# Down projection of a two-layer encoder's FFN: tokens stationary, 512-column weights moving, and a turn of the rows

## The chip, the cores and the metric

The kernel runs on one core of one Trainium2 chip. The metric is the time of one execution on the device in microseconds (us). The engines are named as in the profile: PE is TensorE (matmuls), PEld its loads of stationary tiles, DVE is VectorE, ACT is ScalarE, POOL is GpSimd, which here issues DMAs that add to what lies at their target, and SP is SyncE, which issues the other DMAs.

## What is computed

An encoder of two residual layers over 512 tokens with 1024 features, in float32. Layer 0 mixes tokens by gated linear attention, layer 1 by softmax attention, and each layer ends in a gated FFN with 2816 hidden features and a convolution of width 3 along the tokens. The change touches the FFN's last product alone.

```python
def conv_ffn(h, w_up, w_conv, b_conv, w_down):
    u = h @ w_up                                  # 512 x 1024 by 1024 x 5632
    u = lax.conv_general_dilated(u, w_conv[:, None, :], window_strides=(1,), padding=[(1, 1)],
        dimension_numbers=('NWC', 'WIO', 'NWC'), feature_group_count=u.shape[-1]) + b_conv
    val, gate = jnp.split(u, 2, axis=-1)
    return (jax.nn.silu(gate) * val) @ w_down     # 512 x 2816 by 2816 x 1024

for i in range(DEPTH):                            # DEPTH = 2
    x = x + mixer_i(rmsnorm(x, norm_mix[i]))
    x = x + conv_ffn(rmsnorm(x, norm_ffn[i]), w_up[i], w_conv[i], b_conv[i], w_down[i])
```

## The kernel before

**Number format.** Each float32 operand is split into a high part, rounded to the format that TensorE reads (`wh`, `xt`, `nh`, the first half of a `gu`), and a low part, the rest (`wl` and the others). A product is three matmuls: high by high, high by low, low by high. For a weight ScalarE makes the high part (`wh<-raw`) and VectorE the low part (`wl<-raw,wh`). For the strips named in `LOW_0`, `LOW_1` and `LOW_2`, ScalarE writes the negated high part into `wl` and a DMA on POOL's queue adds the weights to it (`low_dma`), so that VectorE does nothing.

**Layout.** x is kept with features on partitions, 8 chunks of 128 features by 512 tokens (`x[0]` to `x[7]`). In the FFN, x goes to DRAM (`x_home`, tiles `xd`) and its buffers (tag "x") then hold weights, from chunk m = 1 on (`WIDE_AT`) until it comes back (`x_load`, at `BACK_AT` = 20).

**Loops.** `ffn` walks the 22 chunks m of 128 hidden features. `act_up(m)` makes the two up projections, the convolution and the gate. Chunks 4 to 21 are multiplied "by seven" (`SEVEN`): the operands are cut into 2 x 2 blocks, and seven products of sums of blocks take the place of eight. The down projection adds over the hidden features, so it is done in pieces when their gates are there: `down_part` for chunks 0 to 7 within m = 9 and for chunks 8 to 15 within m = 17 (`DOWN_AFTER`), `tail_part` for 16 to 19 behind m = 21, and the two last chunks without the scheme (`rest`). Tokens are cut in two halves of 256 for it; `prepare` makes from two chunks the seven token sums and splits them into `gu` tiles.

**`down_part` before.** For each of four strips n of output features (`NQ`), `product` runs seven products, each over four pairs of chunks with three matmuls, so 7 x 4 x 3 x 4 = 336 in a part. A weight tile of 128 x 128 is stationary and 256 tokens move: 128 x 256 into a half of a PSUM buffer. A strip's weights come in three pieces (`Weights.summed`), whose sums VectorE makes: lines L335, L344 and L346 in the profile, with splits at L338 and L375. ScalarE doubles, negates and copies partial results between PSUM buffers (L1222, L1299, L1309, L1317); VectorE adds them (`add_seven`); the finished 128 x 512 tiles `f` and `g` are added to `x_home` by POOL's DMAs.

**Queues and order.** `Weights.todo` is the list of weight pieces in the order of use. `piece` takes the next one and prepares up to `PA` or `PAW` (4 or 6) pieces ahead; `ahead` issues the loads of the next 3 on SP (`LOADS`). `flush` issues on POOL the adding DMAs that are pending. The order on each engine is fixed when the program is built: a scheduler takes the instructions by rank (`tc.high_priority(n)` raises it) and by when their operands come. PSUM has buffers with the tags "acc", "pt" and "s", two each in these parts, and one "po".

**Behind layer 0's FFN.** `tail_part` finishes the output features in two pairs of strips. `end(c, ...)` adds a finished chunk to `x[c]` on VectorE (L1382), and `nxt.chunk(c)` then starts the next layer's norm for it (`xhl` on ScalarE L520, its low part on VectorE L525, the square on ScalarE L529). ScalarE's negated copies for the second pair of strips are lines L1354 and L1369. In layer 1, `end` stores the output.

## Time and profile before

| what | before |
|---|---|
| median of 3 runs (lowest to highest) | 1075.08 us (1074.94 to 1075.72) |
| the profiled execution's own time | 1075.15 us |
| its span, first to last instruction | 1073.4 us |
| ScalarE's busy share | 73% |
| GpSimd's busy share | 15% |
| mean DMA rate over the span | 163 GB/s |

A group's row reads: line, engine, operation, output<-inputs, shapes, count | busy time in all and the mean of one in ns | idle time ahead of them and what ended it. A matmul's duration counts its whole passage, and several are under way at once; their pitch, the time from one start to the next, is the time that each adds. A chain row reads: start, length, engine, output, line, count. A row of a timeline: start, duration, then the instructions, with idle time ahead in brackets. A window's row: its bounds and length, then PE, PEld, DVE, ACT and POOL busy (instructions), the granted clock, the DMA engines' share and GB/s.

In the profile of before, the down parts of layer 0 lie at about 325 to 365 us and 446 to 487 us, and layer 0's tail at about 542 to 555 us.

### The profile page before, as it was taken

The page shows a single profiled execution, that of the slowest core. Times are in us where ns is not written, and L with a number is a line of the kernel's source. Part 1 is how long each engine was busy: PE and PEld are TensorE (multiplying, and loading weights), DVE is VectorE, ACT ScalarE, POOL GpSimd, SP SyncE. Part 2 cuts the span into 40 slices and gives each one's busy share as a digit, 9 for nine tenths or more (in the row PEclk, how much of TensorE's full clock was granted, in tenths as well). Part 3 has the DMA queues.
Part 4 walks back from the last instruction along what each step waited for, and adds up shares of the span by engine and source line. Part 5 has one row for each costly group of instructions (what it writes and reads, how often), then busy time and mean ns, then how long its engine had stood idle before and what let it go on. Part 6 is the DMA issues. An engine that isn't in the chain of part 4 may idle for free.

```text
span 1073.4 us, 18685 instructions
## 1 busy us (share of the span) xinstructions
PE 1064.8 (99%) x7176; PEld 981.2 (91%) x7176; DVE 940.8 (88%) x1423; ACT 784.1 (73%) x1252; POOL 157.0 (15%) x169
## 2 busy tenths in 40 slices
PE   9999999999999999999999999999999999999998
PEld 8888988888999999999988888788899999999997
DVE  7998968888999999999985578787899999999995
ACT  8679665757886788776784677675888777876783
POOL 0212112011101110010015343001201021001000
PEclk9999999999999999999999999999999999999999
DMA  8844447666554874484668565486756487456562
GB/s 292 193 133 100 116 145 259 223 134 127 147 147 124 208 186 124 117 182 124 225 165 208 123 201 167 148 265 142 143 129 159 115 201 196 125 130 155 149 194 82
DMA packets 75322, 174.57 MB, mean 163 GB/s; under 512 B 6880, under 2 KB 7392, under 8 KB 75232
## 3 DMA queue, kind: packets, MB, share of 16 engines
q1 hardware_dynamic: 50624, 114.23, 31.6%
q0 software_dynamic: 19712, 50.60, 27.1%
q10 hardware_dynamic: 4896, 8.55, 2.2%
q8 instruction: 56, 0.92, 0.3%
q14 instruction: 34, 0.28, 0.1%
HBM read 124.85 MB, written 14.68 MB: 130 GB/s over the span
## 4 chain that ended last, share of the span: by engine, by line
PE 95%; DVE 3%; ACT 1%; DMA 0%; issue 0%; DVEq 0%; ACTq 0%
PE r L1153 52%; PE op L608 8%; PE vg L733 5%; PE up L556 3%; PE up L557 3%; PE up L555 3%; PE kq L665 2%; PE av L582 1%; PE A L555 1%; PE A L557 1%; PE B L557 1%; PE A L556 1%; PE B L555 1%; PE B L556 1%; PE pt L1613 1%; PE o L979 1%
## 5 line engine op out<-in xcount | busy, mean ns | idle before, releaser
L1153 PE MATMUL r<-xt,wh 128*128 128x256 f32 x1152 | 208.0, 282 | 0.0
L1153 PE MATMUL r<-gu,wh 128*128 128x256 f32 x1120 | 202.1, 283 | 0.7 <-ACT r L1369 0.7
L375 DVE TENSOR_TENSOR wl<-raw,wh 128x1024 fp32r<-128x1024 f32 x146 | 176.2, 1217 | 19.3 <-ACT wh L374 18.8
L1153 PEld LDWEIGHTS r<-xt,wh 128*128 128x128 f32 x1152 | 178.9, 191 | 0.2
L374 ACT ACTIVATE wh<-raw 128x1024 fp32r<-128x1024 f32 x146 | 151.1, 1052 | 36.6 <-DVE raw L346 8.3
L1153 PEld LDWEIGHTS r<-gu,wh 128*128 128x128 f32 x1120 | 173.6, 190 | 1.9 <-ACT r L1369 1.1
L1153 PE MATMUL r<-xt,wl 128*128 128x256 f32 x576 | 162.8, 283 | 0.0
L1153 PE MATMUL r<-gu,wl 128*128 128x256 f32 x560 | 156.7, 283 | 0.0
L1153 PE MATMUL r<-nh,wh 128*128 128x256 f32 x432 | 122.6, 284 | 0.0
L1153 PE MATMUL r<-nh,wl 128*128 128x256 f32 x432 | 122.0, 282 | 0.0
L1153 PE MATMUL r<-nl,wh 128*128 128x256 f32 x432 | 121.7, 282 | 0.0
L1153 PEld LDWEIGHTS r<-xt,wl 128*128 128x128 f32 x576 | 109.7, 190 | 0.0
L1153 PEld LDWEIGHTS r<-gu,wl 128*128 128x128 f32 x560 | 106.1, 190 | 0.0
L1153 PEld LDWEIGHTS r<-nh,wh 128*128 128x128 f32 x432 | 82.1, 190 | 0.6
L1153 PEld LDWEIGHTS r<-nl,wh 128*128 128x128 f32 x432 | 82.1, 190 | 0.1
L1153 PEld LDWEIGHTS r<-nh,wl 128*128 128x128 f32 x432 | 82.1, 190 | 0.0
L374 ACT ACTIVATE wh<-sum 128x1024 fp32r<-128x1024 f32 x56 | 59.2, 1056 | 24.1 <-DVE sum L344 17.6
L608 PE MATMUL op<-oT,wh 128*128 128x512 f32 x256 | 72.6, 393 | 0.0
L375 DVE TENSOR_TENSOR wl<-sum,wh 128x1024 fp32r<-128x1024 f32 x56 | 68.2, 1217 | 3.8 <-ACT wh L374 3.8
L324 ACT ACTIVATE wh<-raw 128x1024 fp32r<-128x1024 f32 x46 | 48.4, 1051 | 17.2 <-PE A L556 6.7
L344 DVE TENSOR_TENSOR sum<-raw,raw 128x1024 f32<-128x1024 f32 x50 | 60.8, 1216 | 0.0
L608 PEld LDWEIGHTS op<-oT,wh 128*128 128x128 f32 x256 | 47.4, 188 | 9.7 <-ACT oT L1018 0.3
(304 smaller groups left out, 2577.6 us busy)
## 6 DMA issues: line engine op xcount, KB each, us to landing
raw<-in_w_up_dram SPq DMA_DIRECT2D x78, 512.0 KB, 5.1
raw<-in_w_down_dram SPq DMA_DIRECT2D x44, 512.0 KB, 4.0
wl<-raw POOLq DMA_DIRECT2D x20, 512.0 KB, 5.7
wl<-in_w_up_dram POOLq DMA_DIRECT2D x20, 512.0 KB, 6.6
ring<-p ACTq DMA_DIRECT2D x32, 256.0 KB, 2.6
xw<-in_xw_dram SPq DMA_DIRECT2D x8, 512.0 KB, 6.8
raw<-in_w_v_dram SPq DMA_DIRECT2D x8, 512.0 KB, 4.5
raw<-in_w_g_dram SPq DMA_DIRECT2D x8, 512.0 KB, 4.0
```

The costliest lines, as they stand in the source:

```text
L324: act.activation(hi, r, AF.Copy)
L344: dve.tensor_tensor(fold(e), t3[:, :S].rearrange("p (o n) -> p o n", o=1).to_broadcast([P, 2, S]), fold(tiles[0]), ALU.add)
L374: act.activation(hi[:, sl], a, AF.Copy)
L375: dve.tensor_tensor(lo[:, sl], a, hi[:, sl].bitcast(F32), ALU.subtract)
L555: mm(ps, wh, mh, start=start, stop=False, **kw)
L556: mm(ps, wh, ml, start=False, stop=False, **kw)
L557: return mm(ps, wl, mh, start=False, stop=stop, **kw)
L582: mm(ps[j][:, :width], hl[k][i == 2][:, j * P : (j + 1) * P], (wl if i == 1 else wh)[:, sl], start=k == 0 and i == 0, stop=k == KC - 1 and ...
L608: mm(pss[ng][n], wt[:, sl], mv, start=k == late[0][0] and i == 0, stop=k == late[-1][-1] and i == 2)
L665: mm(ps[t], (wl if i == 1 else wh)[:, kk * S + t * P : kk * S + (t + 1) * P], norm.hl[k][i == 2], start=k == 0 and i == 0, stop=k == KC - ...
L733: last = mm(ps[j], m[:, js], w[:, sl], start=i in (1, 7, 2) and p == 0 and a == 0, stop=i in (4, 2, 3) and p == 3 and a == 2, skip_group_c ...
L1153: mm(dst, w[:, sl], m, start=start and j == 0 and a == 0, stop=j == len(pairs) - 1 and a == 2, skip_group_check=True)
```

## The change

**Down parts.** `down_part` now multiplies with tokens stationary and weights moving. `rows(i, ps, start, hf)` runs one of the seven products over one half hf of the pairs: for two pairs, two groups j of 128 tokens and three terms, a 128 x 128 tile of `gu` is stationary and 512 columns of a weight piece move, into a whole PSUM buffer of 128 tokens by 512 output features. A part has 7 x 2 x 2 x 2 x 3 = 168 matmuls. The seven products stand in the order 1, 7, 6, 4, 5, 2, 3 (`DOWN_ORDER`); the partial results are `ya` (tag "acc"), `yb` ("pt") and `yc` ("s"), and the finished ones `e`, `f` and `g`, which POOL's DMAs store to `y_home` (tiles `yd`, 128 tokens by 1024 features): written by part 0, added by part 1.

**Their weights.** A part has 14 pieces of 128 x 1024 in place of the strips' sums. `load_rows` loads raw blocks as whole rows; `make_rows` adds two of them on VectorE for products 7, 6, 5 and 3 and splits each piece. The two raw tiles of product 1 are in "x" buffers. `_layout` puts the weights in that order ahead of the launch.

**Turning back.** At m = 18 (`Y_AT`) `turn_back` loads the four `yd` tiles on SP. From m = 20 on (`BACK_TURNS`) it gives `product` eight steps, one of which runs after each product: four transposes of 128 x 128 on TensorE into one PSUM buffer `yt` (tag "po"), a copy on ScalarE into `x[c]` at rank 200, and after every second step a DMA on POOL that adds `x_home` to the pair of chunks. The loads of `x_home` into x at m = 20 are gone.

**Behind layer 0.** In `tail_part`, the norm's steps `nxt.chunk(c)` for c = 2 and 3 are kept in `later` and issued behind the next pair's negated copies. The additions in `end` have rank 200 (`END_RANK`).

**Low parts by DMA.** `LOW_0` loses 13 and gains 14 and 16, so one more strip of the up projection in each layer has its low part made by a DMA. `OP_FIRST` and `ROW_DMA` are empty, so what they govern does nothing.

**What moved: the start of part 0 in layer 0.** On TensorE, before, where the first of the part's matmuls stands; r_3231 is the up projection of m = 9, r_3359 the part's first strip and r_3414 the next up projection:

```order
L1153 MATMUL r_3231<-nh_2232,wl_3140 128x256
L1153 MATMUL r_3359<-gu_2374,wh_3211 128x256 x2
L1153 MATMUL r_3414<-gu_2374,wh_3245 128x256 x2
L1153 MATMUL r_3414<-gu_2374,wl_3246 128x256
L1153 MATMUL r_3414<-gu_2575,wh_3245 128x256
L1153 MATMUL r_3359<-gu_2374,wl_3212 128x256
L1153 MATMUL r_3359<-gu_2575,wh_3211 128x256 x2
```

and of the change, where r_3233 is the up projection of m = 9 and ya_3341 the part's first result:

```order
L1202 MATMUL r_3233<-xt_2476,wl_3103 128x256
L1363 MATMUL ya_3341<-wh_3164,gu_2376 128x512
L1202 MATMUL r_3233<-nh_2215,wh_3070 128x256
L1202 MATMUL r_3233<-nl_2216,wh_3070 128x256
L1202 MATMUL r_3233<-nh_2215,wl_3071 128x256
L1363 MATMUL ya_3341<-wl_3165,gu_2376 128x512
L1363 MATMUL ya_3341<-wh_3164,gu_2376 128x512
L1363 MATMUL ya_3341<-wh_3164,gu_2577 128x512
L1363 MATMUL ya_3341<-wl_3165,gu_2577 128x512
```

The matmuls are twice as wide, and the part's first piece (wh_3164, wl_3165) is read among the last products of m = 9.

SP's queue, before, with the loads of part 0 in layer 0:

```order
L270 DMA raw_3070<-in_w_down_dram 128x2x512
L273 DMA raw_3071<-in_w_down_dram 128x2x512
L270 DMA raw_3215<-in_w_down_dram 128x2x512
L273 DMA raw_3216<-in_w_down_dram 128x2x512
L270 DMA raw_3343<-in_w_down_dram 128x2x512
L273 DMA raw_3344<-in_w_down_dram 128x2x512
```

and of the change, where raw_3074 and raw_3106 are product 1's two tiles, in "x" buffers:

```order
L277 DMA raw_3147<-in_w_down_dram 128x1024
L277 DMA raw_3168<-in_w_down_dram 128x1024
L277 DMA raw_3219<-in_w_down_dram 128x1024
L277 DMA raw_3252<-in_w_down_dram 128x1024
L277 DMA raw_3074<-in_w_down_dram 128x1024
L277 DMA raw_3106<-in_w_down_dram 128x1024
L277 DMA raw_3348<-in_w_down_dram 128x1024
```

The pieces used first are loaded fifth and sixth, behind those for products 7 and 6.

**What moved: the turn at m = 20.** TensorE before, in the last products of m = 20 in layer 0, where nothing stands between them:

```order
L1153 MATMUL r_5705<-nh_2225,wl_5558 128x256
L1153 MATMUL r_5705<-nh_2232,wh_5557 128x256
L1153 MATMUL r_5705<-nl_2233,wh_5557 128x256
L1153 MATMUL r_5705<-nh_2232,wl_5558 128x256
L1153 MATMUL r_5705<-nh_2211,wh_5614 128x256
```

and of the change, with the third and fourth group of transposes:

```order
L1223 MATMUL yt_5426<-ident,y_5091 128x128
L1202 MATMUL r_5457<-nh_2229,wh_5244 128x256
L1202 MATMUL r_5457<-nl_2230,wh_5244 128x256
L1202 MATMUL r_5457<-nh_2229,wl_5245 128x256
L1202 MATMUL r_5457<-nh_2236,wh_5244 128x256
L1202 MATMUL r_5457<-nl_2237,wh_5244 128x256
L1202 MATMUL r_5457<-nh_2236,wl_5245 128x256
L1202 MATMUL r_5316<-nh_2215,wh_5168 128x256
L1223 MATMUL yt_5444<-ident,y_5088 128x128
L1223 MATMUL yt_5444<-ident,y_5089 128x128
```

Seven matmuls lie between these two groups, which share one PSUM buffer.

**What moved: layer 0's tail.** ScalarE before, where the negated copies of the second pair of strips stand (r_6218 and r_6226):

```order
L1222 ACTIVATE f_6242<-r_6228 128x512
L337 ACTIVATE wh_6150<-raw_5908 128x512
L1222 ACTIVATE f_6252<-r_6245 128x512
L520 ACTIVATE xhl_6177<-x_5758,prm 128x512
L1369 ACTIVATE r_6218<-r_6168 128x256
L1354 ACTIVATE r_6226<-r_6203 128x256
L520 ACTIVATE xhl_6190<-x_5758,prm 128x512
```

and of the change (r_5865 and r_5873):

```order
L1447 ACTIVATE r_5873<-r_5850 128x256
L569 ACTIVATE xhl_5875<-x_5381,prm 128x512
L1296 ACTIVATE f_5901<-r_5887 128x512
L1296 ACTIVATE f_5911<-r_5904 128x512
L569 ACTIVATE xhl_5881<-x_5381,prm 128x512
L376 ACTIVATE wh_5852<-raw_5768 128x1024
L375 ACTIVATE wl_5853<-raw_5768 128x1024
L375 ACTIVATE wl_5889<-raw_5817 128x1024
L1465 ACTIVATE r_5865<-r_5827 128x256
L1465 ACTIVATE r_5873<-r_5850 128x256
```

The first two copies (L1354 before, L1447 now) stand ahead of the norm's steps (L520, now L569), and the second two (L1369, now L1465) stand together, no longer right behind one of those steps.

The diff, cut to its core:

```diff
@@ -61,6 +61,11 @@
 NQ, NPART = 4, 2
+DOWN_ORDER = (1, 7, 6, 4, 5, 2, 3)
+BACK_TURNS = 20
+Y_AT = 18
+TURN_RANK = 200
 NTAIL = 2
@@ -89,7 +94,7 @@
-LOW_0 = (5, 6, 7, 8, 9, 13, 15, 17)
+LOW_0 = (5, 6, 7, 8, 9, 14, 15, 16, 17)
@@ -104,6 +109,8 @@
 UPAW = 3
+END_RANK = 200
@@ -260,9 +267,51 @@
+        def load_rows(self, src, n, h):
+            part, i = divmod(n, 10)
+            q, key = {1: 0, 7: 1, 6: 2, 5: 1, 2: 3}.get(i), (id(src), n, h)
+            if q is None or key in self.loaded:
+                return
+            self.loaded[key] = t = pair("x", KC // 2, F32, "raw") if i == 1 else pair("raw", NR, F32, "raw")
+            sync.dma_start(t, src[part * NQ + 2 * h + q // 2, :, q % 2 * 2 * S : (q % 2 + 1) * 2 * S])
+        def make_rows(self, src, n, h):
+            self.load_rows(src, n, h)
+            at = lambda i: (id(src), n // 10 * 10 + i, h)
+            put = lambda a, b: dve.tensor_tensor(a, a, b, ALU.add)
+            i, raws = n % 10, self.loaded
+            if i in (1, 2):
+                r = raws[at(i)]
+            elif i in (7, 6):
+                r = raws[at(1)]
+                put(r, raws[at(i)])
+                if i == 7:
+                    del raws[at(7)]
+            elif i == 4:
+                r = raws[at(6)]
+            elif i == 5:
+                r = raws.pop(at(5))
+                put(r, raws.pop(at(6)))
+            else:
+                r = raws.pop(at(2))
+                put(r, raws.pop(at(1)))
+            hi, lo = self.two()
...
+                self.split(hi, lo, r)
+            return hi, lo
         def load(self, key):
             src, i, h = key
-            if i < 0:
+            if i <= -100:
+                self.load_rows(src, -i - 100, h)
+            elif i < 0:
                 self.load_vg(src, -i, h)
@@ -416,10 +468,7 @@
             add_up(layer, range(first, m + 1))
-            W.add(down_w[layer], range(part * NQ, (part + 1) * NQ), 4)
-            at = len(W.todo) - 4 * NQ - 1
-            if m not in SEVEN:
-                W.todo[at : at + 2] = W.todo[at + 1], W.todo[at]
+            W.todo += [(down_w[layer], -100 - 10 * part - i, h) for i in DOWN_ORDER for h in range(2)]
             first = m + 1
@@ -1153,6 +1202,31 @@
             W.flush()
+            if turning:
+                turning.pop(0)()
+        y_home, turning = [dp.tile([P, D], F32, tag=nm("yd"), name=nm("yd")) for _ in range(NT)], []
+        def turn_back():
+            W.flush()
+            y = [big(F32R, "y") for _ in range(NT)]
+            for t, home in zip(y, y_home):
+                sync.dma_start(t.bitcast(F32), home)
+            tiles = []
+            def turned(c):
+                if not tiles:
+                    tiles.extend(x_tiles())
+                ps = bank("po", "yt")
+                for t in range(NT):
+                    pe.transpose(ps[:, t * P : (t + 1) * P].bitcast(F32R), y[t][:, c * P : (c + 1) * P], identr)
+                with tc.high_priority(TURN_RANK):
+                    act.activation(x[c], ps, AF.Copy)
+                if c % 2 == 1:
+                    pool.dma_start(tiles[c // 2], x_home[c // 2], accum_op=ALU.add)
+            return [lambda c=c: turned(c) for c in range(KC)]
@@ -1277,9 +1351,70 @@
             pairs = [quads.pop(part * NQ + i) for i in range(NQ)]
-            st = {}
-            pieces = [{} for _ in range(NQ)]
-            go = lambda n, *a: product(pieces[n], w_dn, part * NQ + n, pairs, *a)
+            near, far = slice(0, S), slice(S, 2 * S)
+            def rows(i, ps, start, hf):
+                wh, wl = W.piece(w_dn, -100 - 10 * part - i, hf, PAW if W.wide else PA)
+                for a in range(2):
+                    mh, ml = pairs[2 * hf + a][i]
+                    for j in range(2):
+                        js = slice(j * P, (j + 1) * P)
+                        for b, (m_, w) in enumerate(((mh, wh), (mh, wl), (ml, wh))):
+                            mm(ps[j], m_[:, js], w[:, a * S : (a + 1) * S], start=start and hf == a == b == 0,
+                               stop=hf == a == 1 and b == 2, skip_group_check=True)
+                    W.flush()
+            def whole(*a):
+                for hf in range(2):
+                    rows(*a, hf)
+            def copied(src, tag, n):
+                t = [tmp(tag, n) for _ in range(2)]
+                for j in range(2):
+                    act.activation(t[j], src[j], AF.Copy)
+                return t
+            def store(t, half, o):
+                for j in range(2):
+                    home = y_home[2 * half + j][:, o]
+                    if part == 0:
+                        pool.dma_start(home, t[j])
+                    else:
+                        W.pending.append((home, t[j]))
+            first = [bank("acc", "ya") for _ in range(2)]
+            rows(1, first, True, 0)
+            yield
+            rows(1, first, True, 1)
+            third = [bank("s", "yc") for _ in range(2)]
+            for j in range(2):
+                act.activation(third[j], first[j], AF.Copy)
+            second = [bank("pt", "yb") for _ in range(2)]
+            whole(7, second, True)
+            f = copied(second, "u", "f")
+            whole(6, first, False)
+            e = copied(first, "t", "e")
+            whole(4, second, False)
+            for j in range(2):
+                dve.tensor_tensor(e[j], second[j], e[j], ALU.subtract)
+            store(e, 0, far)
+            whole(5, first, False)
+            for j in range(2):
+                dve.tensor_tensor(f[j], f[j], first[j], ALU.subtract)
+            store(f, 1, far)
+            whole(2, third, False)
+            store(copied(third, "t", "g"), 0, near)
+            rows(3, first, False, 0)
+            begin_up(m + 1)
+            rows(3, first, False, 1)
+            store(copied(first, "u", "g"), 1, near)
@@ -1288,49 +1423,6 @@
-            begin(0)
-            yield
-            for n in range(NQ):
...
-                W.pending.append((c, g))
@@ -1341,17 +1433,21 @@
                         mm3(ps, cur[0][:, at : at + P], cur[1][:, at : at + P], *plain[FC - 2 + k], False, k == 1, skip_group_check=True)
-                    end(c, ps, n == NQ - 1 and o == 1)
+                    end(c, ps, n == NQ - 1 and o == 1, later if n == 1 else None)
             begin(1)
+            later = []
             for two in ((0, 1), (2, 3)):
                     with tc.high_priority(200):
-                        act.activation(third[n][:, :H], r2(n), AF.Copy, scale=-1.0)
+                        copied = act.activation(third[n][:, :H], r2(n), AF.Copy, scale=-1.0)
+                while later:
+                    with tc.issue_after(copied.ins):
+                        nxt.chunk(later.pop(0))
                 r4 = {}
@@ -1377,10 +1473,13 @@
-        def end(c, ps, last=False):
+        def end(c, ps, last=False, later=None):
             if nxt is not None or not last:
-                dve.tensor_tensor(x[c], x[c], ps, ALU.add)
-                if nxt is not None:
+                with tc.high_priority(END_RANK) if END_RANK else ExitStack():
+                    dve.tensor_tensor(x[c], x[c], ps, ALU.add)
+                if nxt is not None and later is not None:
+                    later.append(c)
+                elif nxt is not None:
                     nxt.chunk(c)
@@ -1394,8 +1493,11 @@
                 W.loads, W.wide = LOADS, 0
-                x_load()
-            elif m == WIDE_AT:
+            if m == Y_AT:
+                back = turn_back()
+            if m == BACK_TURNS:
+                turning += back
+            if m == WIDE_AT:
                 W.loads, W.wide, W.turn = LOADS_FFN, 1, TURN
@@ -1403,6 +1505,9 @@
                     pass
+            while turning:
+                turning.pop(0)()
+                W.flush()
             if m % 2 == 0:
...
```

More of the change, by code (lines that the diff above doesn't have):

```diff
@@ L63 @@
 NQ, NPART = 4, 2
+DOWN_ORDER = (1, 7, 6, 4, 5, 2, 3)
+BACK_TURNS = 20
+ROW_DMA = ()
+Y_AT = 18
+TURN_RANK = 200
 NTAIL = 2
@@ L106 @@
 UPAW = 3
+OP_FIRST = ()
+END_RANK = 200
 PC_NORM = 0
@@ L283, in make @@
             src, i, h = key
+            if i <= -100:
+                self.made[id(src), i, h] = self.make_rows(src, -i - 100, h)
+                return
             if i < 0:
@@ L607, in part @@
                         sl = slice((kk * 2 + n) * P, (kk * 2 + n + 1) * P)
-                        mm(pss[ng][n], wt[:, sl], mv, start=k == late[0][0] and i == 0,
+                        W.op = mm(pss[ng][n], wt[:, sl], mv, start=k == late[0][0] and i == 0,
                            stop=k == late[-1][-1] and i == 2)
@@ new lines, in whole @@
+            def whole(*a):
[11 more added lines that the diff above has]
+                        pool.dma_start(home, t[j])
+                    else:
+                        W.pending.append((home, t[j]))
@@ L1612, in turn @@
                         o = (2 * c + k) * P
-                        pe.transpose(tp[:, k, j * P : (j + 1) * P].bitcast(F32R), ps[j][:, o : o + P], identr)
+                        with tc.issue_after(W.op.ins) if (h, i) in OP_FIRST else ExitStack():
+                            pe.transpose(tp[:, k, j * P : (j + 1) * P].bitcast(F32R), ps[j][:, o : o + P], identr)
                 ph, pl = pts[h][c]
@@ L1734, in _layout @@
     for part in range(NPART):
-        for n in range(0, KC, 2):
+        for i in range(part * NQ, (part + 1) * NQ, 2):
             for odd, d in ((0, 0), (0, 1), (1, 1), (1, 0)):
-                order += [(2 * (part * NQ + i) + odd, n + d) for i in range(NQ)]
+                order += [(2 * (i + a) + odd, d * (KC // 2) + n) for a in range(2) for n in range(KC // 2)]
     whole = order + [(k, n) for n, k in PLAIN]
```

35 lines of the change are left out of this document (5 added, 30 removed).

## The prediction

> **What bounds the kernel now.** I read the page first, its busy shares, slices and chain.
>
> ```profile
> span 1073.4 us, 18685 instructions
> PE 1064.8 (99%) x7176; PEld 981.2 (91%) x7176; DVE 940.8 (88%) x1423; ACT 784.1 (73%) x1252; POOL 157.0 (15%) x169
> DVE  7998968888999999999985578787899999999995
> PEclk9999999999999999999999999999999999999999
> PE 95%; DVE 3%; ACT 1%; DMA 0%; issue 0%; DVEq 0%; ACTq 0%
> ```
>
> TensorE is busy 99% of the span at the full granted clock, and 95% of the chain is its own: time goes where its matmuls go. VectorE stands second with 88%, at nine tenths or more through nearly all of the FFNs. So there are two questions: how long TensorE takes for the new instructions, and whether VectorE, where it is full, still hands over the weights in time. The profiled execution took 1075.15 us, 1.75 more than its span, and 0.07 more than the median of the runs; the sum is made from 1075.15.
>
> **The matmuls of the down parts.** The groups by line and shape:
>
> ```profile
> L1153 PE MATMUL r<-gu,wh 128*128 128x256 f32 x1120 | 202.1, 283 | 0.7 <-ACT r L1369 0.7
> L1153 PE MATMUL r<-gu,wl 128*128 128x256 f32 x560 | 156.7, 283 | 0.0
> ```
>
> Those are 1680 products of 256 columns. A down part has 4 x 7 x 4 x 3 = 336 of them, four parts 1344; the other 336 are the tail's and stay. The new parts issue 7 x 2 x 2 x 2 x 3 = 168 of 512 columns each, 672 in all. A matmul's duration in these rows (283 ns) overlaps its neighbours', so the price is the pitch, from long pieces of the chain in order of time:
>
> ```profile
> 134.00 34.73 PE vg L733 x153
> 187.92 30.26 PE op L608 x133
> 264.66 270.24 PE r L1153 x2256
> 664.61 0.63 PE pt L1613 x8
> 778.36 270.17 PE r L1153 x2256
> ```
>
> 270.24 / 2256 = 119.8 ns for 256 columns. The projections at L733 and L608 have 512 columns and a new stationary tile for each matmul; L733 also has tokens stationary and weights moving, the new form. They give 34.73 / 153 = 227.0 and 30.26 / 133 = 227.5. So 1344 x 0.1198 = 160.9 us become 672 x 0.2270 = 152.5: **-8.4 us**. The arithmetic is the same; what is saved is 12.5 ns for each pair of matmuls made into one. With 227.5 it would be -8.1.
>
> The Trainium skill, page "TensorE: Matmul & The Clock Gate", section "Wait — 56ns, not 53.3ns?", gives the pitch as columns over 2.4 GHz plus a fixed 2.5 ns or so. By it a merged pair saves 2.5 ns, 1.7 us in all by estimate in place of 8.4, and the sum below would come to about 1079. The trace disagrees at 256 columns, where it shows 119.8 and the page would have 109.2. The row decides, since it is of this kernel and 2256 matmuls long.
>
> **Turning the rows back.** The result now has tokens on partitions, and 8 groups of 4 transposes a layer bring it back, 64 new instructions that TensorE did not have. The nearest rows are attention's transposes of the same size, seen in TensorE's timeline in a stretch where a group of four lies between other matmuls:
>
> ```profile
> 679.83 0.46 PE L1613 MATMUL pt<-ident,ring 128*128 128x128 f32 x4
> 680.12 0.70 PE L608 MATMUL op<-oT,wh 128*128 128x512 f32 x2
> 680.65 0.39 PE L555 MATMUL po<-pth,vh 128*128 128x512 f32 x1
> ```
>
> The four take 0.29 us from start to start. The two behind them take 0.53 in place of 2 x 0.227: 0.076 more. That is 0.37 for a group, and the piece of eight above (0.63 us) agrees at 80 ns each. 16 groups x 0.37 = **+5.9 us**; without the 0.076 it would be 4.7. The upper end is a pitch as long as a whole transpose's duration (0.46 - 3 x 0.08, about 0.22): 64 x 0.22 = 14.
>
> The same page, section "Part 4: PE-mode transpose", puts a transpose at about 275 ns in a kernel. That would be 17.6 us by estimate, and a sum of about 1084. The trace's group of eight in 0.63 us speaks against it.
>
> **The waits of the turned rows.** All groups use one PSUM buffer ("po"), so a group waits until ScalarE has copied the one ahead into x. The trace of before has no such pair; its parts are in these two rows of the groups and a piece of the tail, below:
>
> ```profile
> L1222 ACT ACTIVATE r<-r 128x512 f32<-128x512 f32 x60 | 34.9, 582 | 14.7 <-PE r L1153 14.5
> L374 ACT ACTIVATE wh<-raw 128x1024 fp32r<-128x1024 f32 x146 | 151.1, 1052 | 36.6 <-DVE raw L346 8.3
> ```
>
> A copy of 512 columns takes 0.58; with some 0.25 to 0.3 of handover the round trip is 0.85 to 0.9. In the new order 33, 9, 7, 9, 52, 12 and 7 matmuls of 256 columns lie between a layer's groups. Seven are 0.84 us and nine are 1.08, so the four short gaps of a layer cover the round trip barely or just not. What stands between the copies on ScalarE, a halved copy and a gate's copy, ends as the next group does. I take 0.1 for each of eight short gaps: **+0.8**. The ends are nothing (all hidden), and 8 x 0.58 = 4.6 if one other 512-column copy is ahead each time.
>
> **Layer 0's tail.** TensorE's one wait in the FFNs is there; its timeline:
>
> ```profile
> 546.79 0.28 PE L1153 MATMUL r<-gu,wl 128*128 128x256 f32 x1
> 547.76 0.50 PE L1153 MATMUL r<-gu,wh 128*128 128x256 f32 x2 [0.69 <-ACT r L1369]
> ```
>
> and the chain at that place:
>
> ```profile
> 544.30 1.18 DVE wl L375
> 545.48 0.60 DVE wl L338
> 546.08 0.61 DVE x L1382
> 546.71 0.61 ACT xhl L520
> 547.34 0.37 ACT r L1369
> 547.76 3.13 PE r L1153 x24
> ```
>
> The negated copy (L1369) that TensorE needs stands on ScalarE behind a piece of the next layer's norm (L520), which waits for an addition to x that VectorE makes late. The change puts the norm's pieces behind these copies and the additions ahead of weight work. The idle time is 0.69 and the pitch 0.97 for 0.12, 0.85 lost; what is late next is only the next copy. I take **-0.7**, between 0 (the same wait comes one copy later) and -0.85. Layer 1 has no next layer and no such wait.
>
> **VectorE, ScalarE, SP and POOL.** From the groups on VectorE:
>
> ```profile
> L375 DVE TENSOR_TENSOR wl<-raw,wh 128x1024 fp32r<-128x1024 f32 x146 | 176.2, 1217 | 19.3 <-ACT wh L374 18.8
> L375 DVE TENSOR_TENSOR wl<-sum,wh 128x1024 fp32r<-128x1024 f32 x56 | 68.2, 1217 | 3.8 <-ACT wh L374 3.8
> L344 DVE TENSOR_TENSOR sum<-raw,raw 128x1024 f32<-128x1024 f32 x50 | 60.8, 1216 | 0.0
> L338 DVE TENSOR_TENSOR wl<-raw,wh 128x512 fp32r<-128x512 f32 x56 | 38.3, 684 | 2.2 <-ACT y L1210 1.0 <-PE r L1153 0.9
> L346 DVE TENSOR_TENSOR raw<-sum,raw 128x512 f32<-128x512 f32 x56 | 38.3, 683 | 0.4
> L335 DVE TENSOR_TENSOR raw<-raw 128x512 f32<-128x512 f32 x56 | 38.2, 681 | 0.1
> L224 DVE TENSOR_TENSOR raw<-raw,raw 128x1024 f32<-128x1024 f32 x12 | 14.6, 1215 | 0.0
> ```
>
> Gone are 16 each of L344, L346, L335, L338 and the split of a sum: 16 x (1.216 + 0.683 + 0.681 + 0.684 + 1.217) = 71.7 us. New are 32 additions like L224 (38.9) and 26 more splits of 1.217 (31.6; the two low parts a layer given to DMAs and the one taken back are in that count). That is -1.2, all off the path: **0**. ScalarE stands at 73% and its list grows shorter. Its queue has no new place in which a copy waits for a DMA that TensorE needs at once. POOL has 32 stores for 32 additions to DRAM, plus 8 additions into x; SP has 8 loads of y for 8 of x. They lie between m = 18 and the tail, with three chunks of matmuls as cover. If that cover fails, a late y holds TensorE itself, and each us late is one us on the end.
>
> What changes is *when* VectorE works. Windows of both down parts of layer 0 (second and last row) and of what lies ahead of each:
>
> ```profile
> 264.60:325.20 60.60, 60.60 (x507) 60.43 (x506) 58.23 (x86) 51.37 (x80) 5.44 (x5) 1.00 0.54 133
> 325.20:365.20 40.00, 40.00 (x336) 39.94 (x335) 38.45 (x50) 27.37 (x44) 5.89 (x7) 1.00 0.67 168
> 365.20:445.80 80.60, 80.60 (x675) 80.44 (x674) 77.71 (x112) 65.24 (x102) 8.05 (x9) 1.00 0.63 155
> 445.80:486.90 41.10, 41.10 (x347) 41.10 (x346) 40.17 (x53) 28.42 (x45) 6.11 (x7) 1.00 0.65 155
> ```
>
> VectorE is idle 1.5 of 40.0 and 0.9 of 41.1 us in the parts (third figure), and TensorE still never waits. The new order of pieces (1, 7, 6 in two halves) wants 6 splits and 4 additions, 6 x 1.217 + 4 x 1.215 = 12.2 us of VectorE, before the sixth piece, 5 x 12 x 0.227 = 13.6 us in. Before, that stretch holds one strip and a third of the next, about 9.2 us. So 3.0 us of work come earlier; the lead of the weights and the idle 0.9 to 1.5 pay for it. I take 0, with up to 1.5 a part as the other end.
>
> **Sum:** 1075.15 - 8.4 + 5.9 + 0.8 - 0.7 = **1072.7 us**, 0.2% faster. A measurement of this kernel can tell about 0.2% (2.15 us) from no change; the bounds are 1072.9 and 1077.2.
>
> **The rivals.**
>
> (a) *Waits take the gain back.* The copies into x come late behind ScalarE's or VectorE's work, 2 to 4 us over both layers, or VectorE is late by 0.5 a part: 1074 to 1076.5. For it: gaps of 0.84 us against a trip of 0.85 to 0.9, VectorE at its limit. Against it: the copies' high rank.
>
> (b) *Slower: the first weights of a part come late.* The 3.0 us that come earlier, less the 1.5 that was idle, are 1.5 a part, 6 for four: 1078.7. It decides from 1.2 us a part on (1077.2). In part 0 the two loads of product 1's rows also wait for a buffer which TensorE frees 62 matmuls (7.4 us) ahead of their use. The DMA's rows beside the two conversions:
>
> ```profile
> raw<-in_w_up_dram SPq DMA_DIRECT2D x78, 512.0 KB, 5.1
> raw<-in_w_down_dram SPq DMA_DIRECT2D x44, 512.0 KB, 4.0
> ```
>
> 4.0 to 5.1 and 1.05 and 1.22 make 6.3 to 7.4: just in time. Against it: the parts' total on VectorE is smaller than before, and a weight's lead is several pieces.
>
> (c) *All hides.* No waits and 0.29 for a group: 1075.15 - 8.4 + 4.7 - 0.85 = 1070.6.
>
> (d) *The pitches don't carry over*, and the change doesn't save what its count says: a fixed part of 2.5 ns, or transposes at 0.22: 1079 to 1084. The skill's two rules are this case. The trace's 227 and 80 ns are against it.
>
> **Chances.** The forecast with waits of 0 to 1.5 (1071.5 to 1073.5) 0.42; (a) 0.27; (b) 0.10; (c) 0.18; (d) 0.03. Faster by over 0.2% takes (c) and three quarters of the forecast, 0.50. Slower takes (b) and (d), 0.13. The rest, 0.37, is within 0.2%. The range runs from 1069.9 (somewhat under c, as a wait or two more may go) to 1077.2, where (b) begins to decide.
>
> **What would show it.** In the profile after: a piece of 512-column matmuls in the parts at 227 ns, else the first term is wrong; groups of yt at 0.3 to 0.4 us from start to the next matmul's normal pitch; idle time ahead of yt released by ScalarE's copy, under 1.5 us in all, else (a); idle time ahead of ya or yb released by VectorE's wl, none expected, else (b); no wait at the negated copy of the tail. VectorE's share should hold at 88%, TensorE's busy time fall by some 2.5 us. A wait for y's loads at m = 20 would be a mistake of mine about SP and POOL.

## The result, and the profile after

The changed kernel takes **1084.32 us** (median of 6 runs, 1082.60 to 1087.74) beside 1074.95 for the kernel before in the same sessions: a ratio of **1.0085, interval 1.0074 to 1.0096**. It is slower by 9 us, and its runs scatter over 5 us where those of before scatter over 1. The profiled execution took 1084.77, 9.6 more than that of before. Its page:

```profile
span 1083.1 us, 17462 instructions
PE 1068.3 (99%) x6568; PEld 953.1 (88%) x6568; DVE 941.4 (87%) x1401; ACT 774.2 (71%) x1218; POOL 157.0 (14%) x175
PE 76%; DVE 9%; DMA 7%; issue 4%; ACT 4%; POOL 0%; SPq 0%; DVEq 0%; ACTq 0%; POOLq 0%
```

The busy shares hardly moved. The chain did: TensorE's own part of it fell from 95% to 76%, and DMAs went from 0 to 7%. Something else now ends last, at many short places. (The chain says what came last, not what it cost: TensorE is still busy 99% of the span.) The view of TensorE's waits names them (who waits, for whom: sum, times, longest):

```profile
PE r L1202 <- ACT r L1269: 3.0, 3, 1.7
PE r L1202 <- DMA wl<-in_w_up_dram: 0.8, 2, 0.6
PE ya L1363 <- DVE f L1403: 0.5, 1, 0.5
PE ya L1363 <- DVE wl L427: 0.3, 1, 0.3
PE yb L1363 <- ACT wh L426: 0.3, 1, 0.3
```

The view counts only idle time. A wait costs more in pitch, since the pipeline drains: the 1.7 us above is a gap of 2.02 us between two starts that are otherwise 0.12 apart. Counted so on TensorE's timeline, in us above the normal pitch:

| what TensorE waits for | layer 0 | layer 1 |
|---|---|---|
| a copy on ScalarE behind the split of m = 20's weights, which SP loads behind y | 1.18 | 1.90, and 1.50 at half the clock |
| low parts that POOL's DMA adds (strips 9, 14, 15) | 0.80 | 0.25, 0.36, 0.11 |
| the start of part 0, behind product 1's weights | | 0.51, 0.25, 0.48 |
| a negated copy (L1269) at the start of a part | 0.39, 0.26 | |
| the start of part 1: `f` from VectorE in layer 1 | 0.22 | 0.63 |

That is 2.9 and 6.0, together 8.8 us. None of it is in the profile of before.

**How one of them is read.** ScalarE's timeline of the changed kernel in layer 1, ahead of the largest wait:

```profile
1015.18 1.06 ACT L426 ACTIVATE wh<-raw 128x1024 fp32r<-128x1024 f32 x1 [0.37 <-DVE raw L398]
1016.15 1.04 ACT L426 ACTIVATE wh<-sum 128x1024 fp32r<-128x1024 f32 x1
1018.81 1.06 ACT L426 ACTIVATE wh<-raw 128x1024 fp32r<-128x1024 f32 x1 [1.62 <-DMA raw<-in_w_up_dram]
1019.77 0.37 ACT L1269 ACTIVATE r<-r 128x256 f32<-128x256 f32 x1
```

SP's timeline there:

```profile
1006.79 4.97 SPq L1215 DMA_DIRECT2D y<-yd  x3
1011.85 1.32 SPq L319 DMA_DIRECT2D raw<-in_w_up_dram  x1
```

and TensorE's:

```profile
1018.17 0.28 PE L1202 MATMUL r<-nh,wl 128*128 128x256 f32 x1
1020.19 0.39 PE L1202 MATMUL r<-nh,wh 128*128 128x256 f32 x1 [1.74 <-ACT r L1269]
```

SP stands at the loads of y until the last stores of the part have landed. The load of m = 20's weights starts only at 1011.85 and takes 6.9 us, where the page has 5.1 as the median of such loads. ScalarE, whose next instruction splits those weights, stands 1.62 us. The negated copy (L1269) that TensorE needs is ready to run, but stands behind that split. TensorE waits for a 0.37 us copy whose own inputs were there.

### The profile page after: what moved, and what is told of

Its sections match the earlier page's. It is cut to its first block, busy times and chain, and to the rows that moved or that the text cites. A ratio compares the mean times of both kernels' runs of the same rounds, so it can differ in the third digit from the quotient of the medians.

```text
span 1083.1 us, 17462 instructions
## 1 busy us (share of the span) xinstructions
PE 1068.3 (99%) x6568; PEld 953.1 (88%) x6568; DVE 941.4 (87%) x1401; ACT 774.2 (71%) x1218; POOL 157.0 (14%) x175
## 4 chain that ended last, share of the span: by engine, by line
PE 76%; DVE 9%; DMA 7%; issue 4%; ACT 4%; POOL 0%; SPq 0%; DVEq 0%; ACTq 0%; POOLq 0%
PE r L1202 29%; PE op L657 8%; PE vg L782 5%; PE ya L1363 5%; DVE wl L427 3%; PE up L605 3%; PE up L604 3%; PE up L606 3%; DMA raw<-in_w_up_dram 2%; PE yb L1363 2%; DMA wl<-in_w_up_dram 2%; ACT wh L426 1%; PE yc L1363 1%; DMA raw<-in_w_down_dram 1%; PE A L604 1%
## 5 line engine op out<-in xcount | busy, mean ns | idle before, releaser
L426 ACT ACTIVATE wh<-raw 128x1024 fp32r<-128x1024 f32 x172 | 177.5, 1054 | 74.5 <-DVE raw L283 34.5
L427 DVE TENSOR_TENSOR wl<-raw,wh 128x1024 fp32r<-128x1024 f32 x172 | 206.8, 1219 | 22.9 <-ACT wh L426 22.1
L1363 PE MATMUL ya<-wh,gu 128*128 128x512 f32 x256 | 83.5, 392 | 0.5 <-DVE f L1403 0.5
L415 POOL DMA_DIRECT2D wl<-in_w_up_dram x22 | 23.0, 1047 | 247.4 <-ACT wl L375 182.0
L376 ACT ACTIVATE wh<-raw 128x1024 fp32r<-128x1024 f32 x44 | 46.3, 1051 | 17.1 <-PE A L605 7.0
L1363 PEld LDWEIGHTS ya<-wh,gu 128*128 128x128 f32 x256 | 48.1, 188 | 11.3 <-DVE f L1403 0.7
L426 ACT ACTIVATE wh<-sum 128x1024 fp32r<-128x1024 f32 x40 | 42.2, 1056 | 12.6 <-PE r L1202 3.4
L1363 PE MATMUL ya<-wl,gu 128*128 128x512 f32 x128 | 50.3, 393 | 0.3 <-DVE wl L427 0.3
L427 DVE TENSOR_TENSOR wl<-sum,wh 128x1024 fp32r<-128x1024 f32 x40 | 48.8, 1221 | 1.8 <-ACT wh L426 1.7
L1284 ACT ACTIVATE y<-u,cw 128x512 f32<-128x512 f32 x48 | 38.9, 811 | 15.4 <-DVE u L1299 11.2
```

The costliest lines, as they stand in the source:

```text
L376: act.activation(hi, r, AF.Copy)
L415: pool.dma_start(lo.bitcast(F32) if same else lo, r, accum_op=ALU.add)
L426: act.activation(hi[:, sl], a, AF.Copy)
L427: dve.tensor_tensor(lo[:, sl], a, hi[:, sl].bitcast(F32), ALU.subtract)
L1284: act.activation(y, u, AF.Identity, scale=w(1), bias=w(3))
L1363: mm(ps[j], m_[:, js], w[:, a * S : (a + 1) * S], start=start and hf == a == b == 0, stop=hf == a == 1 and b == 2, skip_group_check=True)
```

## The experiments

Each was run with five rounds beside the kernel before; ratios are to the kernel before. "After" is the changed kernel with 1.0085.

**1. The loads of y on POOL's queue (y_pool).**

```diff
-                sync.dma_start(t.bitcast(F32), home)
+                pool.dma_start(t.bitcast(F32), home)
```

> Only the queue of the four loads of y changes: POOL in place of SP. Theory 1 (a queue's order): on SP these loads wait for the last stores of the part and hold the loads of m = 20's weights behind them; ScalarE then stands at the split of those weights, and the negated copy that TensorE needs stands behind it. The two waits there (1.18 us at 501.7 and 1.90 us at 1018.2 in the profile of the change) and the stretch of matmuls at 213 ns behind the second (1.7 us) go: about -4.7 us, near 1079.6. Theory 2 (VectorE and ScalarE are full, and the waits move to whatever comes last): under 1.5 us, 1083 or more, with a new wait within the next 10 us.

1081.13 us, 1.0059 [1.0046, 1.0072]: about 2.8 less than after. ScalarE's timeline in that kernel:

```profile
1016.25 1.04 ACT L426 ACTIVATE wh<-sum 128x1024 fp32r<-128x1024 f32 x1
1017.19 1.04 ACT L426 ACTIVATE wh<-raw 128x1024 fp32r<-128x1024 f32 x1
1018.14 0.36 ACT L1269 ACTIVATE r<-r 128x256 f32<-128x256 f32 x1
```

The split no longer waits, the wait of 1.90 is gone with the slow stretch behind it, and that of layer 0 is 0.36 for 1.18. So the cause is right at its place. The gain is smaller than 4.7. In this profile low parts came later, which takes 1.3 us of it back:

```profile
PE r L1202 <- DMA wl<-in_w_up_dram: 2.3, 3, 0.8
```

**2. LOW_0 as before (low_old).**

```diff
-LOW_0 = (5, 6, 7, 8, 9, 14, 15, 16, 17)
+LOW_0 = (5, 6, 7, 8, 9, 13, 15, 17)
```

> Only LOW_0 as before: strip 13's low part by a DMA again, those of 14 and 16 by VectorE. Theory 1: the three waits of TensorE on low parts of strips 14 and 15 that POOL's DMA adds (0.80 us at 410.2, 0.36 at 926.9, 0.11 at 937.4) go, about -1.3 us, near 1083.0. Theory 2 (VectorE sets the pace around the down parts): one more split of 1.22 us a layer on VectorE costs up to 2.4 us, 1084 to 1087, with longer waits on VectorE's wl and on copies behind it at the starts of the parts.

1081.46, 1.0061 [1.0049, 1.0073]: about 2.6 less than after. The waits at strip 14 are gone, and the extra split costs 0.2 us a layer at most, behind VectorE at the start of part 1. But the waits at 501.7 and 1018.2 are gone too, and new ones stand 15 us ahead of them. ScalarE's timeline in this kernel, and then TensorE's:

```profile
483.76 0.58 ACT L1374 ACTIVATE g<-ya 128x512 f32<-128x512 f32 x1
487.56 0.60 ACT L1374 ACTIVATE g<-ya 128x512 f32<-128x512 f32 x1 [3.21 <-DMA yd<-f]
488.05 0.38 ACT L1260 ACTIVATE r<-r 128x256 f32<-128x256 f32 x1
```

```profile
488.48 0.50 PE L1202 MATMUL r<-xt,wh 128*128 128x256 f32 x2 [1.30 <-ACT r L1260]
```

The copy of the second `g` needs a buffer of tag u. There are three, and two hold `f` until POOL's store of them has landed. ScalarE stands 3.21 us, and TensorE's copy again stands behind it: a second wait of the same kind. In after ScalarE stood only 0.54 and 0.58 us at this copy, and TensorE not at all.

**3. Both together (y_low), and then the last `g` in another buffer (y_low_gt).**

```diff
-            store(copied(first, "u", "g"), 1, near)
+            store(copied(first, "t", "g"), 1, near)
```

> Two edits together: the loads of y by POOL and LOW_0 as before; TURN stays 1. Theory 1 (separate waits in the engines' queues): the two gains seen alone add up, 1084.3 - 3.2 - 2.8 = 1078.3. Theory 2 (ScalarE and VectorE have no slack there, so a wait taken away shows up again behind): 1080 or more.

1081.43, 1.0055 [1.0042, 1.0067]: no better than either alone, as theory 2 said. The profile shows the reason, waits of 1.15 and 1.04 us behind that copy at 486.8 and 1004.1, and one of 0.57 five us behind each, all four gone in the next run's profile.

> As the run before, and the last two tiles g of a part are copied into buffers of tag t (five) in place of u (three). With LOW_0 as before, ScalarE's copy of the second g stood 3.2 us because the u buffers were held by the tiles f until POOL's stores of them had landed, and the negated copy behind it cost TensorE 1.46 us at 486.9 and 1.20 at 1002.8. Theory 1 (a store's landing holds a buffer, the buffer holds ScalarE's queue): those two waits go, 2 to 2.6 us under the run before. Theory 2: the gates' y use the same tag, and the wait only changes its name: within 0.7 us of the run before.

**1078.81, 1.0034 [1.0022, 1.0047]**, 2.6 under the run before it, as theory 1 expected. ScalarE's timeline in this kernel has the same copy, which stood 3.21 us in low_old:

```profile
484.10 0.60 ACT L1374 ACTIVATE g<-ya 128x512 f32<-128x512 f32 x1 [0.18 <-DMA yd<-g]
```

So what looked like saturation in y_low was one more named wait. With three causes gone, 5.5 of the 9 us are back. The profiled execution was the lowest of the six, 1075.65: no low part is late in it, and it takes 0.5 us more than that of before. What the other five, 1077.90 to 1079.73, wait for has not been seen.

**4. Without the turn (no_turn), and without those waits too (gt_nt).** Edit of no_turn; gt_nt adds the edits of 2 and 3:

```diff
                 W.loads, W.wide = LOADS, 0
-            if m == Y_AT:
-                back = turn_back()
-            if m == BACK_TURNS:
-                turning += back
+                x_load()
```

> Leaves out the turn: no loads of y, no transposes, no copies into x, and x comes back by SP's loads at m = 20 as before, so what the parts computed is not added. Measures what the turn costs in all. Theory 1: 16 groups of transposes at 0.40 (6.4 us), TensorE's waits on the copies into x (0.6) and the waits that the loads of y caused on SP (4.7): 11.7 less, near 1072.6. Theory 2 (the waits come from full ScalarE and VectorE, not from y): the transposes and their waits alone, 7 less, near 1077.

1074.21, 0.9989 [0.9980, 0.9998], 10.1 under after: nearer to theory 1 (11.7) than to theory 2 (7).

> As no_turn (leaves out the turn, so what the parts computed is not added), with LOW_0 as before and the last g in tag t. What is left of the change are the wide matmuls and the tail's edit, with the known waits taken away but for those at part 0's start. Theory 1 (merged matmuls save 12 ns a pair, 7.4 to 8.4 us in all, and the rest was waits): 1075.0 - 7.7 - 0.8 + 1.5 = 1068. Theory 2 (the wide matmuls save nothing to speak of in this kernel): 1073 or more.

**1071.39, 0.9963 [0.9951, 0.9976].** It lies between the two, 3.7 us under before. Against y_low_gt, which differs by the turn and little else, it is 7.4 us less: that is the whole price of 64 transposes, their copies and waits. In its profiled execution, 1069.78, the two FFNs are 4.3 us shorter than before's; the smaller matmul term measured below (-6.4), the tail (-0.85) and the waits that are left (+2.6) make -4.7.

**5. Product 1's raw tiles (turn0, gt_turn2, gt_nosum).** ScalarE's timeline of after at the start of part 0 in layer 1:

```profile
834.67 1.06 ACT L426 ACTIVATE wh<-raw 128x1024 fp32r<-128x1024 f32 x1 [2.01 <-DMA raw<-in_w_down_dram]
835.63 0.58 ACT L1296 ACTIVATE u<-r 128x512 f32<-128x512 f32 x1
```

The tile that ScalarE stands for is product 1's, whose load waits for an x buffer. SP issues it at 829.22, when TensorE has freed that buffer, and it lands 5.4 us later. The 0.39 in layer 0 is something else. TensorE's timeline there, and then ScalarE's:

```profile
320.72 0.39 PE L1363 MATMUL ya<-wh,gu 128*128 128x512 f32 x1
321.34 0.39 PE L1202 MATMUL r<-nh,wh 128*128 128x256 f32 x1 [0.23 <-ACT r L1269]
```

```profile
320.92 0.37 ACT L1269 ACTIVATE r<-r 128x256 f32<-128x256 f32 x1 [0.56 <-PE r L1202]
```

ScalarE's copy waits for TensorE's own product, and one wide matmul is all that covers it. The wait is 0.39 in all seven profiles with this order on TensorE (after, y_pool, low_old, y_low, y_low_gt, no_turn, gt_nt).

Two kernels shift which pieces take these buffers:

```diff
-TURN = 1
+TURN = 0
```

> Only the phase changes in which weight pieces take the x buffers (TURN 0 for 1): by the order of the program, from the last read of the buffer for product 1's first raw tile to the first use of its weights there are 20.4 us in part 0 in place of 7.4, and in part 1 11.8 in place of 20.4. Theory 1 (that buffer comes free too late in part 0): the waits at 320.7 (0.39), 836.3 (0.51), 838.1 (0.25) and 841.5 (0.48) go, about -1.6 us, near 1082.7, and none comes in part 1. Theory 2 (VectorE is what is late there): no change within 0.5 us, the same waits on wl and on ScalarE's copies.

1081.74, 1.0063 [1.0047, 1.0079], which overlaps after's interval. The four waits are gone, that in layer 0 because six wide matmuls now stand where one stood. But others came: 0.61 behind VectorE's wl at 327.9 and at 844.3, 0.50 and 0.49 at the start of part 1, where theory 1 had none, and 1.47 and 1.81 for strip 9's low part. Together with edits 1 and 2 (three):

> The three edits together: y by POOL, LOW_0 as before, TURN 0. Theory 1: the waits are apart in time and add up, -4.7 - 1.3 - 1.6 = -7.6 us, near 1076.7. Theory 2: what is won at one place is waited for at the next, 1081 or more.

1083.79, 1.0081 [1.0068, 1.0094]: nothing is left of the gains. ScalarE's and VectorE's pieces at the starts of both parts cost 0.6 to 1.0 each, and strip 9's low part 1.54 and 1.63. Theory 1's sum fell here.

> As y_low_gt (y by POOL, LOW_0 as before, last g in tag t), with TURN 2 for 1. By the order of the program the time between the x buffer's last read and the first use of product 1's weights is then 11.8 us in part 0 (7.4 with TURN 1) and 7.4 in part 1 (20.4). Theory 1 (the release of that buffer sets the wait): TensorE's waits at the start of part 0 (0.39 at 320 us, 0.5 to 1.5 between 836 and 842 us in the four profiles with TURN 1) go, and waits of 0.4 to 1.5 us come at the start of part 1 (near 440 and 958 us). Theory 2 (VectorE is late at these places): the waits stay at part 0's start. In time the two give nearly the same, within 1.5 us of 1078.8; the place tells them apart.

TURN 2 on y_low_gt: 1090.09, 1.0139 [1.0125, 1.0152]. Waits came at part 1's start (0.53 and 0.29, then 0.39), but those at part 0 stayed (0.49 and 0.32, then 0.49 and 0.34), so the place doesn't decide. The largest loss is in the low parts, 5.3 us in pitch; the rest is spread, some of it ahead of the parts:

```profile
PE r L1202 <- DMA wl<-in_w_up_dram: 4.8, 3, 2.5
```

Then VectorE was relieved instead:

```diff
                 r = raws[at(1)]
-                put(r, raws[at(i)])
```

> As y_low_gt, but leaves out VectorE's additions for products 7 and 6 of the down parts (their weights are then wrong, and nothing else changes): 16 additions, 19.4 us of VectorE, 4.9 of them in the first third of each part. Theory A (the raw tile of product 1 lands late because its buffer comes free late): the waits at part 0's start stay, 0.39 near 320 us and about 0.5 near 838 us, since that tile's load waits for TensorE and not for VectorE; part 1's short waits behind wl (0.13 to 0.2) go. Theory B (VectorE's work that the change brings forward is what is late): all waits at the starts of the parts go, and the time falls by 1.5 to 3 us, to 1076 to 1077.

1081.16, 1.0051 [1.0038, 1.0063], 2.3 *more* than y_low_gt with 19.4 us less on VectorE. Theory B's gain didn't come, but the edit does more than was meant: product 7's raw tile is then read by nothing, so its buffer comes free sooner. Between 313 and 319 us SP issues five loads of down weights where y_low_gt has three, and they land in 7.8 us (median) in place of 5.0. New waits of TensorE stand at 437.4, 491.8 and 1007.6 (1.02, 1.03 and 0.99), the first behind a wait of ScalarE of 3.38 for such a load. So this run does not clear VectorE. The wait in layer 1 stayed (0.53 at 837.8), with ScalarE's row

```profile
834.35 1.06 ACT L425 ACTIVATE wh<-raw 128x1024 fp32r<-128x1024 f32 x1 [1.28 <-DMA raw<-in_w_down_dram]
```

and that in layer 0 went, as eight wide matmuls stand there now. How much of layer 1's wait is the buffer's release, how much the load's own time and how much VectorE stays open. A separate buffer for the tile was not tried.

**6. The small edits on the kernel before (b_tail, b_low, b_both).** b_tail has `later` and the rank in `end`; b_low has the new LOW_0; b_both has both.

```diff
-                    end(c, ps, n == NQ - 1 and o == 1)
+                    end(c, ps, n == NQ - 1 and o == 1, later if n == 1 else None)
...
+                while later:
+                    with tc.issue_after(copied.ins):
+                        nxt.chunk(later.pop(0))
...
-                dve.tensor_tensor(x[c], x[c], ps, ALU.add)
+                with tc.high_priority(200):
+                    dve.tensor_tensor(x[c], x[c], ps, ALU.add)
```

> The kernel before with the tail's edit alone: later and the rank of the additions in end. Theory 1: the wait of 0.85 us at 546.8 goes: 1074.2 to 1074.5. Rival: the norm's steps that are put off are late themselves and the next layer's first matmuls wait: 1075 or more.

1074.27, 0.9992 [0.9983, 1.0001]: the size that was expected, with an interval that just reaches 1; its profile has no wait at that copy. (It has one of 0.83 at 363.2, where the edit touches nothing.)

> The kernel before with the new LOW_0 alone. Theory 1 (a low part that POOL's DMA adds comes too late for strip 14 whatever the down parts are): TensorE waits on wl by 0.3 to 0.9 us in m = 14 of each layer, 1075.5 to 1077. Rival (it is late only because the new down parts hold VectorE, ScalarE and the raw buffers longer): no wait, 1074.5 to 1075.3.

1074.32, 0.9994 [0.9985, 1.0003]: not to be told from no change. The profiled run, at 1076.02, has one late low part, on TensorE's timeline

```profile
403.22 0.39 PE L1153 MATMUL r<-nh,wl 128*128 128x256 f32 x1 [1.17 <-DMA wl<-in_w_up_dram]
```

so strip 14's low part can come late without the new down parts as well, in some executions.

> The kernel before with the tail's edit and the new LOW_0, without the new down parts. Alone they gave medians of 1074.27 and 1074.32 beside 1075.05. If they add up: 1073.5, and its interval lies under 1. Rival: the low part of strip 14 that came 1.33 us late in one profile comes late more often: 1074.3 or more.

**1074.03, 0.9987 [0.9978, 0.9997].** It is the only version that computes everything and whose interval lies under 1, just, by 1.4 us.

## Why the prediction was wrong

By its own terms, for the profiled executions:

| term | forecast | measured |
|---|---|---|
| 672 wide matmuls for 1344 | -8.4 | -6.4 |
| 16 groups of transposes | +5.9 | +5.8 |
| waits of the turned rows | +0.8 | +1.3 |
| layer 0's tail | -0.7 | -0.85 |
| ScalarE, VectorE, SP, POOL | 0 | +8.8 |
| sum | -2.4 | +8.7 |

The profiles differ by 9.6. By TensorE's first matmul of each stage, the two FFNs are 2.6 and 6.6 us longer, the attention between them is 0.7 shorter, and 1.15 lie behind the last matmul, where the last store of the output lands later. Up to the first FFN they agree within 0.1. So 0.5 of the FFNs' 9.2 us are not in the sum; I have not followed them up.

**The step that failed** is the sentence on ScalarE: "Its queue has no new place in which a copy waits for a DMA that TensorE needs at once." There were three. Splits of m = 20's weights wait for a load that SP issues behind y (shown by y_pool); with the slow stretch behind them they are 4.6 of the 8.8 us. The split of product 1's weights waits for a load into a late buffer: 1.2 us in layer 1 (seen in the profiles, not isolated). The copy of the last `g` waits for a store to free its buffer; it cost TensorE nothing in after, and 2.7 in low_old, where the order had moved (shown by y_low_gt). I counted ScalarE's share, 73% and falling, where the order in its queue decided. SP was dismissed in the same breath: I weighed only that y itself could be late for TensorE, not who stands behind y in SP's queue. Of POOL I counted the DMAs and not when they land: late low parts are 1.5 us (low_old has 0.25 of them). The last 1.5 are the two negated copies, the 0.22 and `f`.

**VectorE** was the wrong suspect. Rival (b) had the right sign, the start of part 0 as a place and even the 7.4 us between release and use, but it put its price on VectorE's 3.0 us of early work, with 0.10 for a chance. The parts' starts cost 2.7 us, and only a part of it stood behind VectorE. The other half of (b) did happen in layer 1: the load and the two conversions, 5.43 + 1.06 + 1.22 = 7.7 us, did not fit into the 7.1 from the buffer's release at 829.22 to the first use at 836.31. gt_nosum had no gain from less work on VectorE, but it moved the loads too.

**The matmuls** saved as they should, at a smaller size. Some pieces of the chain of after:

```profile
327.45 3.94 PE ya L1363 x17
341.24 5.06 PE yb L1363 x22
346.30 5.45 PE ya L1363 x24
351.75 5.53 PE yc L1363 x24
```

These have 231.8, 230.0, 227.1 and 230.4 ns a matmul; all eleven such pieces between 321.95 and 364.24 come to 37.47 us for 163, or 229.9. I had taken 227.0 from one piece of another stage. The other three parts have 229 to 230 as well, without their waits. 672 x 2.9 ns are the missing 2 us. The 2.5 ns a merged pair of rival (d) would have saved 1.7 us in place of 6.4, so the trace's order of size stands. Rival (d)'s upper sum, 1084, meets the measured time by luck: it took the transposes for three times what they cost.

**The transposes** were right to a tenth. From the chain of after, in layer 1:

```profile
1032.11 0.30 PE yt L1223 x4
1032.41 0.90 PE r L1202 x7
1033.31 0.39 PE yt L1223 x4
```

A group takes 0.30, the seven matmuls behind it 0.90 in place of 0.84: 0.36. Sixteen are 5.8. The next group shows 0.09 of the wait for ScalarE's copy. Such remainders, eight groups of 0.37 in place of 0.30, make 0.6, and the gaps ahead of the groups, the larger ones 0.28, 0.14, 0.06 and 0.14, make 0.7: the waits are 1.3 for my 0.8. **The tail** was right too: b_tail isolates it with -0.76, in an interval that just reaches 1.

So even with every other wait gone, the change is the difference of large terms, -6.4 for the matmuls and +7.1 for the turn, and the tail's -0.85: nothing, to a tenth or two. It had nothing to pay for a wait with.

## What to carry to other kernels

On an engine that works in order, a busy share says nothing about whether a copy comes in time: list, for each copy that the bound engine needs, what stands ahead of it and which DMA, buffer or store that waits for. When a change moves loads to the head of a queue, ask who stands behind them, and follow that reader to its own queue. Where a wait is taken away and the time doesn't move, look in the profile for the next named wait before calling an engine full: y_low looked like saturation until one buffer tag was changed.

## What the hardware showed

A wait of TensorE can cost more than itself. Windows of after around the wait of 1.74 us, TensorE's granted clock being the third figure from the right:

```profile
1020.10:1021.40 1.30, 1.21 (x10) 1.21 (x11) 1.30 (x2) 1.07 (x3) 0.00 (x0) 1.00 0.73 233
1021.40:1024.80 3.40, 3.40 (x19) 3.40 (x18) 0.54 (x2) 0.88 (x2) 0.00 (x0) 0.51 0.18 65
1025.00:1033.00 8.00, 8.00 (x71) 7.90 (x70) 7.82 (x11) 6.04 (x12) 0.87 (x1) 1.00 0.21 68
```

From 1.3 us behind the wait's end, the clock was half for 3.4 us (0.51 in the second row), with 213 ns a matmul in place of 120, which cost another 1.50 us. The Trainium skill, page "TensorE: Matmul & The Clock Gate", section "Part 1: The HAM clock gate (the "warmup" mystery)", has half the clock after an idle window of about 3.4 us, with windows that run freely. The 3.4 us agree; but here a wait of 1.74 was enough, while one of 2.5 in gt_turn2 was not followed by a slower clock:

```profile
316.30:317.50 1.20, 1.09 (x9) 1.09 (x10) 0.99 (x2) 0.00 (x0) 0.00 (x0) 1.00 1.04 423
317.50:321.00 3.50, 3.50 (x32) 3.50 (x31) 1.52 (x3) 3.10 (x5) 0.00 (x0) 1.00 0.86 350
```

The traces have a reading that fits these two. In all fifteen profiles the granted clock changes only at whole multiples of 3.413 us from its first full grant: at 298 and 299 of them in after, at 311 to 317 at the ends. Cut at this grid, after's wait lies whole in one window (1018.05 to 1021.46), half of which is idle. That of 2.5 us in gt_turn2 falls into two windows, with 1.31 and 1.23 idle; another there, 1.64 us at 834.5, lies whole in one and was not followed by a slower clock either. So what counts may be how much of one window is idle, and not how long the wait is. It is not shown: there is one case with a slow stretch, and behind the last matmul of before a window with 1.77 us idle was not followed by half the clock, though matmuls' ends in a profile are modelled.

The scatter is open as well. The runs of the changed kernel lie 5.1 us apart and those of the variants with the new parts 1.7 to 6.1, where 22 runs of before lie 3.2 apart, 1.4 without the highest. That waits for DMAs make the difference is not shown.
